# One decoder layer on one core: score products not pinned, the mixers' norm weight spread by products, first loads rearranged

## The chip, the core and the metric

The kernel runs on one core of a Trainium2 chip. The time is that of one execution on the device in microseconds; three runs of the kernel before gave 1481.52 to 1482.3, median 1482.07. The core has five engines, each with an instruction stream of its own that it works off in order: PE (products and transposes), ACT (activations and copies), DVE and POOL (element-wise work) and SP, which here issues loads. They wait for each other through semaphores. SP, ACT and POOL each feed a DMA queue; all three are served by the same sixteen DMA engines.

## What is computed

A hybrid decoder layer on 512 tokens of width 1024: RMSNorm, one input projection whose columns are split between four retention heads and a sliding-window attention with eight query heads, an output projection, then a mixture of 32 experts (four for each token), an embedding gate and a last RMSNorm. Cut to the part that matters here:

```python
hn = rmsnorm(h, g_mix_norm[i])
u = hn @ w_in[i] + b_in[i]
rq, rk, rv, rg, aq, ak, av = split_cols(u, IN_SIZES)
ret = retention(rq, rk, rv, positions)     # rope on q and k, chunks of 128 tokens
ret = jax.nn.silu(rg) * rmsnorm(ret, ret_norm_g[i])
att = sliding_window_attention(aq, ak, av, att_sinks[i], rel_bias_table)
h = h + jnp.concatenate([ret, att], axis=-1) @ w_out[i]
h = h + moe(rmsnorm(h, g_moe_norm[i]), ...)
```

## The kernel before

The mixers take the first 240 us or so; the mixture of experts behind them takes nearly all the rest and is not touched. All of the mixers works on four tiles of 128 tokens.

*Start.* The four tiles of x (`xt`) and the norm's weight `g_mix`, which a DMA spreads from one row over 128 partitions, come in by SP's queue, and so do the weights. A weight piece (`raw`, 128x2048, 1 MB) is loaded by `prefetch()` into one of three buffers as soon as one is free; the list `pieces` gives their order: two pieces of head 0, one of the attention's keys and values (`w_kv`), two of its queries, two for each further head. In the order of SP's queue stand x's tile 0, g_mix, piece 0, x's tile 1, piece 1, x's tiles 2 and 3, `w_kv`. For each tile ACT sums the squares (L287), DVE makes the factor 1/rms from it in a chain of small operations (L257 to L273, with a square root on ACT) and the normalised tile xn (L362); PE transposes it in two halves (L301), and ACT and DVE take each half out of PSUM, ACT as a rounded part `act_h` (L292) and DVE as the remainder `act_l` (L293).

*Weights* are split in the same manner: ACT writes the rounded part `wh` (L151), DVE the remainder `wl` (L152), for head 0 in quarters of 128x512, else as a whole. A product is made of three: wh by act_h, wh by act_l and wl by act_h.

*Rotary tables* (`rotary_tables`, L436 to L464): DVE works out the angles from the positions in 18 operations, and ACT takes the sine and cosine.

*A retention head* (`retention(h)`, L523): two weight pieces; then for two groups of two tiles each: 24 products a tile (L316) into one of two PSUM buffers (`mm`), DVE adds the bias into `u` (L538, which frees the buffer), POOL makes the sine part of the rotation `rb` (L546), DVE the cosine part and their sums `ra` (L549, L554), PE transposes ra (L558), ACT evicts it (L560); scores and state on PE (L575, L583), score times values (L578), queries times the state before (L580: the cross product); squares on ACT (L593), a chain of fourteen small operations on DVE to `y` (L257 to L598, with the gate: Silu on ACT, L566, times the norm's weight `rng_b` on POOL, L567), two transposes of y (L601) and their eviction.

*The attention* (`attention_in`, L408; `attention(nb)`, L466) works by blocks of 128 queries. For each half of the heads four score products of depth 64 (L482) are made, two of them on the lower and two on the upper half of the partitions (kv = 0, 1), into one PSUM tile for each half; `tc.issue_after` pins each behind the one before, so that the halves alternate. DVE, ACT (Exp) and PE do the softmax and the product with the values.

The program calls head 0, the attention's inputs, block 0, head 1, blocks 1 and 2, head 2, block 3, head 3. The framework's scheduler sets the order of each engine's instructions from the program by costs and due times of its own; `tc.issue_after(x)` adds that what is issued inside stands behind x.

Of the kernel before, what the change touches and what calls it, by code (L numbers as in the profile page):

```python
# [11 lines left out]
F32 = mybir.dt.float32  # L12
# [83 lines left out]
def hymba_kernel(ctx, tc, x, p, positions, rel_bias_table, g_mix_norm, w_in, b_in, ret_norm_g,  # L96
# [58 lines left out]
    def w_half(w, k0, c0):  # L155
        def load(t):
            nc.sync.dma_start(out=t.rearrange("p (k c) -> p k c", k=4),
                              in_=w[k0 * P:(k0 + 4) * P, c0:c0 + 512].rearrange("(k p) c -> p k c", p=P))
        return load
# [2 lines left out]
        nc.sync.dma_start(out=t.rearrange("p (k c) -> p k c", k=8),  # L162
                          in_=w_in[:, 2560:2816].rearrange("(k p) c -> p k c", p=P))

    def w_ret(h, k0):
        def load(t):
            tv = t.rearrange("p (k s c) -> p k s c", k=4, s=4)
            src = w_in[k0 * P:(k0 + 4) * P, :].rearrange("(k p) c -> p k c", p=P)
            for s in range(4):
                c0 = s * 512 + h * P  # L170
                nc.sync.dma_start(out=tv[:, :, s, :], in_=src[:, :, c0:c0 + P])
        return load

    def expert_of(w, t):
# [22 lines left out]
        nc.sync.dma_start(out=t.rearrange("p (k c) -> p k c", k=2),  # L197
                          in_=w_ple_proj.rearrange("(k p) c -> p k c", p=P))

    pieces = [w_ret(0, 0), w_ret(0, 4), w_kv, w_half(w_in, 0, 2048), w_half(w_in, 4, 2048)]  # L200
    for h in range(1, HR):
        pieces += [w_ret(h, 0), w_ret(h, 4)]
    n_first = len(pieces)
# [14 lines left out]
    def prefetch(after=None):  # L218
        if free and state["next"] < min(len(pieces), state["limit"]):
            t, pl_ = raw_tile()  # L220
            if after is not None:
                nc.scalar.activation(t[:, 0:1], after[:, 0:1], AF.Copy)
            pieces[state["next"]](t)
            queue.append((t, pl_))
            state["next"] += 1

    def next_piece(parts=None, dst=None, more=True):
        t, pl_ = queue.pop(0)
        r = split(t, parts, dst)
        free.append(pl_)  # L230
        if more:
            prefetch()
        return r
# [9 lines left out]
    def bcast(pl_, src, n, name, eng=None, bufs=1):  # L243
        t = pl_.tile([P, n], F32, name=name, bufs=bufs)
        (eng or nc.gpsimd).dma_start(out=t, in_=src.rearrange("(o n) -> o n", o=1).broadcast_to([P, n]))
        return t
# [48 lines left out]
    def split_t(tp, src, hi, lo, n=KD):  # L295

        for g in range(0, n, 4):
            m = min(4, n - g)
            t = tp.tile([P, 4, P], F32, name="tp")
            for j in range(m):  # L300
                R.tr = nc.tensor.transpose(out=t[:, j, :], in_=src[:, (g + j) * P:(g + j + 1) * P], identity=ident)  # L301
            ins = split_ps(t[:, 0:m, :], hi[:, g:g + m, :], lo[:, g:g + m, :])
        return ins
# [39 lines left out]
    n1 = pool(nx, "n1", 2)  # L343
    xts = [n1.tile([P, D], F32, name="xt", bufs=NT) for _ in range(NT)]
    nc.sync.dma_start(out=xts[0], in_=x_v[:, 0, :])
    g_mix = bcast(n1, g_mix_norm[0], D, "g_mix", nc.sync)
    prefetch()
    nc.sync.dma_start(out=xts[1], in_=x_v[:, 1, :])
    prefetch()
    for i in range(2, NT):  # L350
        nc.sync.dma_start(out=xts[i], in_=x_v[:, i, :])
    warm = small.tile([P, 1], F32, name="warm", bufs=1)
    nc.vector.memset(warm, 1.0)
    nc.scalar.activation(warm, warm, AF.Sqrt)
    nc.scalar.dma_start(out=cst[:, P:C_REV], in_=consts[:, P:C_REV])
    nc.gpsimd.dma_start(out=pos_i, in_=positions[0].rearrange("(i p) -> p i", p=P))
    sink_b = bcast(const, att_sinks[0], 8, "sink_b")

    for i in range(NT):
        r = rstd(sumsq(xts[i], n1.tile([P, D], F32, name="xn")), D, 1, table=True)  # L360
        xn = n1.tile([P, D], F32, name="xn")
        nc.vector.scalar_tensor_tensor(xn, in0=xts[i], scalar=r, in1=g_mix, op0=ALU.mult, op1=ALU.mult)  # L362
        split_t(tp, xn, xh[:, :, i * P:(i + 1) * P], xl[:, :, i * P:(i + 1) * P])
    prefetch()
    nx.close()

# [8 lines left out]
    av = at.tile([P, NT, P], F32, name="av")  # L375
    aqT = at.tile([P, 4, S], F32, name="aqT")
    rng_b = rp.tile([P, 512], F32, name="rng_b", bufs=1)
    nc.gpsimd.dma_start(out=rng_b, in_=ret_norm_g.rearrange("o h d -> o (h d)").broadcast_to([P, 512]))

    def side_tables():  # L380

# [84 lines left out]
    def attention(nb):  # L466
        nk = 1 if nb == 0 else 2
        k0 = max(nb - 1, 0) * P
        o_sb = at2.tile([P, 512], F32, name="o_sb", bufs=1)
        o_ps = flat(oap.tile([P, 4, P], F32, name="o_ps")).rearrange("p (h d) -> p h d", d=64)  # L470
        sm = small.tile([P, 8], F32, name="sm")
        mx = small.tile([P, 8], F32, name="mx")
        nmx = small.tile([P, 8], F32, name="nmx")
        kvs = [slice(kv * 64, kv * 64 + 64) for kv in range(2)]
        for gp in range(2):

            s_ps = [sps.tile([P, 512], F32, name="s_ps").rearrange("p (a b) -> p a b", a=2) for _ in range(2)]
            m = None
            for g in range(2):
                for kv, rows in enumerate(kvs):  # L480
                    with tc.issue_after(m.ins) if m is not None else nullcontext():
                        m = nc.tensor.matmul(s_ps[kv][:, g, 0:nk * P], lhsT=aqT[rows, gp * 2 + g, nb * P:(nb + 1) * P],  # L482
                                             rhs=akT[rows, k0:k0 + nk * P], start=True, stop=True)
            for kv, rows in enumerate(kvs):
                h0 = kv * 4 + gp * 2
                h2_ = slice(h0, h0 + 2)
                s_sb = at2.tile([P, S], F32, name="s_sb").rearrange("p (a b) -> p a b", a=2)
                nc.vector.scalar_tensor_tensor(
                    s_sb[:, :, 0:nk * P], in0=s_ps[kv][:, :, 0:nk * P], scalar=0.125,
                    in1=band[:, h2_, 256 - nk * P:256], op0=ALU.mult, op1=ALU.add)  # L490
                nc.vector.tensor_reduce(out=mx[:, h2_], in_=s_sb[:, :, 0:nk * P], op=ALU.max, axis=AX.X)
                nc.vector.tensor_tensor(out=mx[:, h2_], in0=mx[:, h2_], in1=sink_b[:, h2_], op=ALU.max)
                nc.vector.tensor_scalar(nmx[:, h2_], mx[:, h2_], -1.0, None, op0=ALU.mult)
                for g in range(2):
                    c = h0 + g
                    nc.scalar.activation(s_sb[:, g, 0:nk * P], s_sb[:, g, 0:nk * P], AF.Exp, bias=nmx[:, c:c + 1],
                                         accum_out=sm[:, c:c + 1])
                t = tp.tile([P, 4, P], F32, name="tp")
                for g in range(2):
                    for kb in range(nk):  # L500
                        nc.tensor.transpose(out=t[:, g * nk + kb, :], in_=s_sb[:, g, kb * P:(kb + 1) * P], identity=ident)
                pT = at2.tile([P, 512], F32, name="pT").rearrange("p (a b) -> p a b", a=4)
                nc.any.tensor_copy(out=pT[:, 0:2 * nk], in_=t[:, 0:2 * nk])
                for g in range(2):
                    for kb in range(nk):
                        nc.tensor.matmul(o_ps[:, h0 + g, :], lhsT=pT[:, g * nk + kb, :],
                                         rhs=av[:, k0 // P + kb, rows], start=(kb == 0), stop=(kb == nk - 1))
        es = small.tile([P, 8], F32, name="es")
        nc.vector.tensor_tensor(out=es, in0=sink_b, in1=mx, op=ALU.subtract)
        nc.scalar.activation(es, es, AF.Exp)  # L510
        nc.vector.tensor_tensor(out=es, in0=es, in1=sm, op=ALU.add)
        nc.vector.reciprocal(out=es, in_=es)
        nc.vector.tensor_tensor(out=o_sb.rearrange("p (h d) -> p h d", d=64), in0=o_ps,
                                in1=es.rearrange("p (h o) -> p h o", o=1).broadcast_to([P, 8, 64]), op=ALU.mult)
        split_t(tp, o_sb, mix[nb][0][:, 4:8, :], mix[nb][1][:, 4:8, :], n=4)
# [6 lines left out]

    def retention(h):  # L523
        bias = rp.tile([P, 4, P], F32, name="bias")
        nc.gpsimd.dma_start(out=bias, in_=b_v[:, :, h * P:(h + 1) * P].broadcast_to([P, 4, P]))
        fine = [(lambda t, k=k: kslice(t, k), lambda t, k=k: kslice(t, k)) for k in range(4)] if h == 0 else None
        ws = [next_piece(fine), next_piece(fine)]
        r_prev = None
        for grp in range(2):
            i0 = grp * 2  # L530
# [12 lines left out]
            rbv = rb.rearrange("p i (a t d) -> p i a t d", a=2, t=2)  # L543
            i2 = slice(i0, i0 + 2)
            for t_o, t_i in ((0, 1), (1, 0)):
                nc.gpsimd.tensor_tensor(  # L546
                    out=rbv[:, :, :, t_o, :], in0=uv[:, :, :, t_i, :],
                    in1=sin[:, i2].rearrange("p i (o d) -> p i o d", o=1).broadcast_to([P, 2, 2, 64]), op=ALU.mult)
            nc.vector.tensor_tensor(  # L549
                out=ra.rearrange("p i (a d) -> p i a d", a=4), in0=u[:, :, 0:256].rearrange("p i (a d) -> p i a d", a=4),  # L550
                in1=cos[:, i2].rearrange("p i (o d) -> p i o d", o=1).broadcast_to([P, 2, 4, 64]), op=ALU.mult)
# [50 lines left out]
            for ii in range(2):  # L602
                split_ps(t[:, ii, :], mix[i0 + ii][0][:, h, :], mix[i0 + ii][1][:, h, :])

    rotary_tables()
    retention(0)
    side_tables()
    attention_in()
# [685 lines left out]
```

## Time and profile before

| | |
|---|---|
| median of three runs | 1482.07 us |
| the profiled execution's own time | 1484.27 us |
| its span | 1482.5 us |
| PE busy | 1352.3 us, 91% of the span |
| DVE busy | 830.4 us, 56% |
| ACT busy | 683.7 us, 46% |
| POOL busy | 211.1 us, 14% |
| mean granted clock of TensorE | 0.958 of full |
| PE busy, tenths, in the first eight of 40 slices | 5 9 9 9 9 8 7 9 |
| the same in the other 32 | 6 once, 8 three times, else 9 |

A slice is 37 us. The profiled execution took 2.2 us longer than the median of the runs; 1.8 us of its time lie around the span. Times in the rows below count from the start of the span.

### The profile page before, as it was taken

The page shows a single profiled execution, that of the slowest core. Times are in us where ns is not written, and L with a number is a line of the kernel's source. Part 1 is how long each engine was busy: PE and PEld are TensorE (multiplying, and loading weights), DVE is VectorE, ACT ScalarE, POOL GpSimd, SP SyncE. Part 2 cuts the span into 40 slices and gives each one's busy share as a digit, 9 for nine tenths or more (in the row PEclk, how much of TensorE's full clock was granted, in tenths as well). Part 3 has the DMA queues.
Part 4 walks back from the last instruction along what each step waited for, and adds up shares of the span by engine and source line. Part 5 has one row for each costly group of instructions (what it writes and reads, how often), then busy time and mean ns, then how long its engine had stood idle before and what let it go on. Part 6 is the DMA issues. An engine that isn't in the chain of part 4 may idle for free. (4 is left out here: it accounts for less than half of the span.)

```text
span 1482.5 us, 16876 instructions
## 1 busy us (share of the span) xinstructions
PE 1352.3 (91%) x6090; PEld 906.2 (61%) x6091; DVE 830.4 (56%) x1013; ACT 683.7 (46%) x754; POOL 211.1 (14%) x227
## 2 busy tenths in 40 slices
PE   5999987969899999999999999999999999999896
PEld 4776766757466564746555666474765675674275
DVE  6637663678456372645455656373664584573157
ACT  5334442356346262535445546263563563553154
POOL 2214130366201000000000000000000000100011
PEclk9999997979999999999999999999999999999998
DMA  9431036688799999999999999999999999999541
GB/s 272 119 108 29 1 116 245 206 281 338 292 401 390 410 399 410 399 395 402 399 386 404 391 380 391 395 398 375 401 380 369 365 385 367 362 347 365 199 147 57
DMA packets 110427, 462.47 MB, mean 312 GB/s; under 512 B 10830, under 2 KB 29180, under 8 KB 77568
## 3 DMA queue, kind: packets, MB, share of 16 engines
q1 hardware_dynamic: 99584, 436.24, 75.4%
q0 software_dynamic: 10320, 24.52, 6.6%
q8 instruction: 49, 0.80, 0.2%
q10 hardware_dynamic: 432, 0.57, 0.1%
q14 instruction: 42, 0.34, 0.1%
HBM read 447.26 MB, written 18.73 MB: 314 GB/s over the span
## 5 line engine op out<-in xcount | busy, mean ns | idle before, releaser
L152 DVE TENSOR_TENSOR wl<-raw,wh 128x2048 fp32r<-128x2048 f32 (+2 forms) x246 | 531.2, 2197 | 138.8 <-ACT wh L151 134.2
L151 ACT ACTIVATE wh<-raw 128x2048 fp32r<-128x2048 f32 (+2 forms) x246 | 444.3, 1839 | 108.4 <-PE up L854 55.8
L874 PE MATMUL up<-raw,xTh 128*64 128x512 f32 x896 | 198.6, 599 | 0.7 <-ACT xTh L823 0.7
L906 DVE TENSOR_SCALAR a<-up 128x512 f32<-128x512 f32 x50 | 34.5, 691 | 285.9 <-ACT sg L905 285.3
L854 PE MATMUL up<-wh,xTh 128*128 128x512 f32 x576 | 162.9, 404 | 14.5 <-ACT wh L151 13.0
L905 ACT ACTIVATE sg<-up 128x512 f32<-128x512 f32 x50 | 29.8, 597 | 302.8 <-issue 130.0
L854 PE MATMUL up<-wl,xTh 128*128 128x512 f32 x576 | 160.8, 400 | 2.3 <-DVE wl L152 2.3
L854 PE MATMUL up<-wh,xTl 128*128 128x512 f32 x576 | 160.9, 401 | 1.4 <-DVE xTl L293 1.4
L874 PEld LDWEIGHTS up<-raw,xTh 128*64 128x64 f32 x896 | 63.5, 138 | 126.8 <-issue 118.4
L854 PEld LDWEIGHTS up<-wh,xTh 128*128 128x128 f32 x576 | 108.1, 191 | 45.7 <-ACT wh L151 18.3
L854 PEld LDWEIGHTS up<-wl,xTh 128*128 128x128 f32 x576 | 108.6, 190 | 33.2 <-DVE wl L152 7.5
L854 PEld LDWEIGHTS up<-wh,xTl 128*128 128x128 f32 x576 | 109.7, 191 | 28.8 <-DVE xTl L293 2.1
L938 PE MATMUL dn<-wh,aTh 128*128 128x512 f32 x288 | 99.5, 429 | 23.1 <-ACT wh L151 23.1
L938 PE MATMUL dn<-wl,aTh 128*128 128x512 f32 x288 | 103.6, 444 | 12.4 <-DVE wl L152 12.4
L874 PE MATMUL dn<-raw,aT 128*64 128x512 f32 x448 | 104.8, 607 | 3.1 <-PEq L1055 3.1
L952 POOL DMA_INDIRECT acc<-y,slot_i x30 | 45.5, 1515 | 432.4 <-ACT y L947 418.9
L807 POOL DMA_INDIRECT xe<-xg,slot_i x30 | 34.0, 1132 | 503.4 <-PE dn L867 240.6
L938 PE MATMUL dn<-wh,aTl 128*128 128x512 f32 x288 | 97.5, 422 | 0.0
L938 PEld LDWEIGHTS dn<-wh,aTh 128*128 128x128 f32 x288 | 58.2, 207 | 42.1 <-ACT wh L151 26.6
L938 PEld LDWEIGHTS dn<-wl,aTh 128*128 128x128 f32 x288 | 58.1, 212 | 30.3 <-DVE wl L152 17.2
L947 ACT ACTIVATE y<-dn,slots 128x1024 f32<-128x1024 f32 (+1 forms) x30 | 27.5, 916 | 98.6 <-PE dn L938 52.3
L924 DVE SCALAR_TENSOR_TENSOR aTl<-tp,aTh 128x512 fp32r<-128x512 f32 x36 | 23.9, 688 | 81.1 <-ACT aTh L923 81.1
(340 smaller groups left out, 1598.4 us busy)
## 6 DMA issues: line engine op xcount, KB each, us to landing
raw<-in_w_up_dram SPq DMA_DIRECT2D x256, 1024.0 KB, 14.7
raw<-in_w_down_dram SPq DMA_DIRECT2D x128, 1024.0 KB, 12.9
raw<-in_w_in_dram SPq DMA_DIRECT2D x32, 256.0 KB, 3.9
raw<-in_w_out_dram SPq DMA_DIRECT2D x4, 1024.0 KB
raw<-in_w_ple_gate_dram SPq DMA_DIRECT2D x4, 1024.0 KB, 11.6
raw<-in_w_in_dram SPq DMA_DIRECT2D x3, 1024.0 KB, 5.2
xt<-in_x_dram SPq DMA_DIRECT2D x4, 512.0 KB, 8.5
h<-in_x_dram POOLq DMA_DIRECT2D x4, 512.0 KB, 5.7
```

The lines of the kernel that those rows point to most:

```text
L151: R.split_act = nc.scalar.activation(to(wh), src(raw), AF.Copy)
L152: R.split_dve = nc.vector.tensor_tensor(out=to(wl), in0=src(raw), in1=to(wh).bitcast(F32), op=ALU.subtract)
L807: return nc.gpsimd.indirect_dma_start(out=dst[0:n, 0:D // h], out_offset=None, in_=xg.rearrange("s (h d) -> (s h) d", h=h), in_offset=bass ...
L854: nc.tensor.matmul(h[n // 2][:, n % 2 * 512:n % 2 * 512 + 512], lhsT=a[:, k, :], rhs=w[:, n * 512:(n + 1) * 512], start=(k == 0 and a is x ...
L874: R.pair = nc.tensor.matmul(o[v * 64:v * 64 + 64, c:c + 512], lhsT=xT[:, k, :], rhs=w[:, v * n + c:v * n + c + 512], start=False, stop=las ...
L905: nc.scalar.activation(sg, hv[:, :, 0], AF.Silu, scale=ALPHA)
L906: nc.vector.tensor_scalar(a[:, cs], hv[:, :, 1], LIMIT + 1.0, 1.0 - LIMIT, op0=ALU.min, op1=ALU.max)
L924: nc.vector.scalar_tensor_tensor(flat(l[:, g4, :]), in0=flat(t), scalar=1.0 / ALPHA, in1=flat(h[:, g4, :]).bitcast(F32), op0=ALU.mult, op1 ...
L938: m = nc.tensor.matmul(o[:, n * 512:(n + 1) * 512], lhsT=a[:, k, :], rhs=w[:, kk * 1024 + n * 512:kk * 1024 + (n + 1) * 512], start=False, ...
L947: nc.scalar.activation(y[:, 0:o.shape[1]], o, AF.Copy, scale=gate)
L952: nc.gpsimd.indirect_dma_start(out=acc.rearrange("s (h d) -> (s h) d", h=h), out_offset=bass.IndirectOffsetOnAxis(ap=idx[0:n, :], axis=0), ...
```

## The change

1. *Norm weight.* The row g_mix_norm is loaded once to one partition (`g_row`); two products with a row of ones (L360 of the changed kernel) spread it into PSUM, and ACT copies it to `g_mix` (L361).
2. *Two queues.* Head 0's second weight piece is loaded by POOL's queue in four DMAs; x's tiles 1 to 3 stand directly behind the first piece on SP's queue.
3. *Loads behind the first rotation.* The loads of `rng_b` and of head 1's bias, on POOL's queue, are issued after head 0's first rotation (`R.rot`).
4. *Pins at the start.* The rotary tables stand behind xn of tile 0 (`R.xn`), the splits of head 0's weights behind the evictions of tile 0 (`R.x_hi`, `R.x_lo`).
5. *Scores.* The pins between the score products are gone.

```diff
-    def w_ret(h, k0):
+    def w_ret(h, k0, eng=None):
...
-                nc.sync.dma_start(out=tv[:, :, s, :], in_=src[:, :, c0:c0 + P])
+                (eng or nc.sync).dma_start(out=tv[:, :, s, :], in_=src[:, :, c0:c0 + P])
...
-    pieces = [w_ret(0, 0), w_ret(0, 4), w_kv, w_half(w_in, 0, 2048), w_half(w_in, 4, 2048)]
+    pieces = [w_ret(0, 0), w_ret(0, 4, nc.gpsimd), w_kv, w_half(w_in, 0, 2048), w_half(w_in, 4, 2048)]
...
-    g_mix = bcast(n1, g_mix_norm[0], D, "g_mix", nc.sync)
+    g_row = n1.tile([1, D], F32, name="g_row", bufs=1)
+    nc.sync.dma_start(out=g_row, in_=g_mix_norm[0].rearrange("(o n) -> o n", o=1))
     prefetch()
-    nc.sync.dma_start(out=xts[1], in_=x_v[:, 1, :])
-    prefetch()
-    for i in range(2, NT):
+    for i in range(1, NT):
         nc.sync.dma_start(out=xts[i], in_=x_v[:, i, :])
...
+    one = n1.tile([1, P], F32, name="one", bufs=1)
+    nc.vector.memset(one, 1.0)
+    g_mix = n1.tile([P, D], F32, name="g_mix", bufs=1)
+    for c in range(2):
+        ps = mm.tile([P, 512], F32, name="mm")
+        nc.tensor.matmul(ps, lhsT=one, rhs=g_row[:, c * 512:(c + 1) * 512], start=True, stop=True)
+        nc.scalar.activation(g_mix[:, c * 512:(c + 1) * 512], ps, AF.Copy)
     nc.gpsimd.dma_start(out=pos_i, in_=positions[0].rearrange("(i p) -> p i", p=P))
+    prefetch()
...
+        if i == 0:
+            R.xn, R.x_lo, R.x_hi = m, m2, R.hh
...
-    nc.gpsimd.dma_start(out=rng_b, in_=ret_norm_g.rearrange("o h d -> o (h d)").broadcast_to([P, 512]))
...
-            m = None
             for g in range(2):
                 for kv, rows in enumerate(kvs):
-                    with tc.issue_after(m.ins) if m is not None else nullcontext():
-                        m = nc.tensor.matmul(s_ps[kv][:, g, 0:nk * P], lhsT=aqT[rows, gp * 2 + g, nb * P:(nb + 1) * P],
-                                             rhs=akT[rows, k0:k0 + nk * P], start=True, stop=True)
+                    nc.tensor.matmul(s_ps[kv][:, g, 0:nk * P], lhsT=aqT[rows, gp * 2 + g, nb * P:(nb + 1) * P],
+                                     rhs=akT[rows, k0:k0 + nk * P], start=True, stop=True)
...
-        nc.gpsimd.dma_start(out=bias, in_=b_v[:, :, h * P:(h + 1) * P].broadcast_to([P, 4, P]))
+        with tc.issue_after(R.rot.ins) if h == 1 else nullcontext():
+            nc.gpsimd.dma_start(out=bias, in_=b_v[:, :, h * P:(h + 1) * P].broadcast_to([P, 4, P]))
...
-        ws = [next_piece(fine), next_piece(fine)]
+        with tc.issue_after(R.x_lo.ins), tc.issue_after(R.x_hi.ins):
+            ws = [next_piece(fine), next_piece(fine)]
...
+            if h == 0 and grp == 0:
+                with tc.issue_after(R.rot.ins):
+                    nc.gpsimd.dma_start(out=rng_b, in_=ret_norm_g.rearrange("o h d -> o (h d)").broadcast_to([P, 512]))
...
-    rotary_tables()
+    with tc.issue_after(R.xn.ins):
+        rotary_tables()
```

With these the scheduler orders the mixers anew on all engines. In three places the order is shown as the program has it.

ACT at the start, before (xt is a tile of x, tp a transposed half, raw a weight piece):

```order
L287 ACTIVATE xn,ss<-xt 128x1024
L259 ACTIVATE rs_y_146<-rs_v_145 128x1
L655 ACTIVATE sel<-cst 128x2
L151 ACTIVATE wh<-raw 128x512
L292 ACTIVATE act_h<-tp 128x4x128
L151 ACTIVATE wh<-raw 128x512
L292 ACTIVATE act_h<-tp 128x4x128
L287 ACTIVATE xn,ss<-xt 128x1024
```

and now:

```order
L287 ACTIVATE xn,ss<-xt 128x1024
L259 ACTIVATE rs_y_155<-rs_v_154 128x1
L667 ACTIVATE sel<-cst 128x2
L361 ACTIVATE g_mix<-mm 128x512 x2
L287 ACTIVATE xn,ss<-xt 128x1024
L259 ACTIVATE rs_y_183<-rs_v_182 128x1
L292 ACTIVATE act_h<-tp 128x4x128 x2
L287 ACTIVATE xn,ss<-xt 128x1024
L151 ACTIVATE wh<-raw 128x512 x2
```

The sum of tile 1 and its square root have moved ahead of the evictions of tile 0, and the sum of tile 2 ahead of the first weight split; before, the first weight split stood directly behind tile 0's square root.

DVE around head 0's first u, before:

```order
L152 TENSOR_TENSOR wl<-raw,wh 128x512
L266 SCALAR_TENSOR_TENSOR rs_t_203<-rs_y_202,rs_v_201 128x1
L152 TENSOR_TENSOR wl<-raw,wh 128x512
L272 TENSOR_SCALAR rs_t_203<-rs_t_203 128x1
L273 TENSOR_TENSOR rs_y_202<-rs_y_202,rs_t_203 128x1
L362 SCALAR_TENSOR_TENSOR xn<-xt,rs_y_202,g_mix 128x1024
L538 TENSOR_TENSOR u<-mm,bias 128x512
L152 TENSOR_TENSOR wl<-raw,wh 128x2048
```

and now (qkT, y, sin and cos are the rotary tables' tiles here):

```order
L465 SCALAR_TENSOR_TENSOR sin<-y,qkT 128x256
L464 TENSOR_SCALAR y<-y 128x256
L466 SCALAR_TENSOR_TENSOR sin<-y,sin 128x256
L465 SCALAR_TENSOR_TENSOR cos<-y,qkT 128x256
L467 SCALAR_TENSOR_TENSOR sin<-y,sin 128x256
L466 SCALAR_TENSOR_TENSOR cos<-y,cos 128x256
L470 TENSOR_SCALAR sin<-sin 128x256
L467 SCALAR_TENSOR_TENSOR cos<-y,cos 128x256
L546 TENSOR_TENSOR u<-mm,bias 128x512
L469 TENSOR_SCALAR cos<-cos 128x256
L546 TENSOR_TENSOR u<-mm,bias 128x512
```

The first two u stood among the weight remainders, behind the normalised tile 2, with the rotary tables long done; now all four tiles, all remainders and sixteen of the eighteen rotary operations stand ahead of them.

PE at head 3, from the cross product (or_ps<-r_prev,qkT) to the second transposes of ra, before:

```order
L580 MATMUL or_ps<-r_prev,qkT 128x128
L316 MATMUL mm<-wh,act_h 128x512
L316 MATMUL mm<-wh,act_l 128x512 x4
L316 MATMUL mm<-wl,act_h 128x512 x4
L601 MATMUL tp<-cst,y 128x128 x2
L558 MATMUL tp<-cst,ra 128x128 x4
```

and now:

```order
L591 MATMUL or_ps<-r_prev,qkT 128x128
L316 MATMUL mm<-wl,act_h 128x512 x3
L316 MATMUL mm<-wh,act_h 128x512 x4
L316 MATMUL mm<-wh,act_l 128x512 x4
L316 MATMUL mm<-wl,act_h 128x512 x4
L316 MATMUL mm<-wh,act_h 128x512 x4
L316 MATMUL mm<-wh,act_l 128x512
L612 MATMUL tp<-cst,y 128x128 x2
L316 MATMUL mm<-wh,act_l 128x512 x3
L316 MATMUL mm<-wl,act_h 128x512 x4
L569 MATMUL tp<-cst,ra 128x128 x4
```

Nine products stood between the cross product and y's transposes and none behind these; now twenty stand between and seven behind. At head 2 it was 20 products between and none behind, and is 27 and none.

## Rows read from the trace of the kernel before

**Rows 1.** Busy time by stretch: us, engines busy (count), PEclk, DMA share, GB/s.

```profile
0.00:10.00 10.00, 0.00 (x0) 0.01 (x1) 1.28 (x11) 2.94 (x7) 5.71 (x18) 1.00 0.81 227
10.00:20.00 10.00, 4.73 (x13) 3.18 (x14) 7.96 (x26) 4.57 (x10) 0.00 (x0) 1.00 1.11 321
...
180.00:190.00 10.00, 10.00 (x45) 7.00 (x44) 4.71 (x21) 1.80 (x8) 0.00 (x0) 0.83 0.00 0
```

**Rows 2.** ACT timeline, the start: start us, us, line, tiles, [idle before <-releaser].

```profile
4.53 1.06 ACT L287 ACTIVATE xn<-xt 128x1024 f32<-128x1024 f32 x1 [1.83 <-DMA xt<-in_x_dram]
...
14.82 0.63 ACT L151 ACTIVATE wh<-raw 128x512 fp32r<-128x512 f32 x1 [5.40 <-DMA raw<-in_w_in_dram]
```

**Rows 3.** DVE timeline, the start.

```profile
8.80 0.24 DVE L439 CAST pos_f<-pos_i 128x4 f32<-128x4 int32 x1 [7.91 <-DMA pos_i<-in_positions_dram]
...
13.66 0.42 DVE L458 SCALAR_TENSOR_TENSOR cos<-y,cos 128x256 f32<-128x256 f32 x1
...
27.28 1.28 DVE L362 SCALAR_TENSOR_TENSOR xn<-xt,rs_y,g_mix 128x1024 f32<-128x1024 f32 x1
28.48 0.68 DVE L538 TENSOR_TENSOR u<-mm,bias 128x512 f32<-128x512 f32 x1
29.08 2.28 DVE L152 TENSOR_TENSOR wl<-raw,wh 128x2048 fp32r<-128x2048 f32 x1
31.28 1.28 DVE L293 TENSOR_TENSOR act_l<-tp,act_h 128x512 fp32r<-128x512 f32 x2
```

**Rows 4.** PE timeline, head 0 and the key/value products.

```profile
33.46 1.09 PE L316 MATMUL mm<-wh,act_h 128*128 128x512 f32 x4
34.39 1.10 PE L316 MATMUL mm<-wh,act_l 128*128 128x512 f32 x4
...
40.37 0.63 PE L558 MATMUL tp<-cst,ra 128*128 128x128 f32 x4 [0.46 <-DVE act_l L293]
...
44.18 0.39 PE L580 MATMUL or_ps<-r_prev,qkT 128*128 128x128 f32 x2
...
55.83 0.63 PE L558 MATMUL tp<-cst,ra 128*128 128x128 f32 x4 [1.46 <-DVE ra L554]
...
59.76 0.39 PE L580 MATMUL or_ps<-r_prev,qkT 128*128 128x128 f32 x2
...
64.51 0.41 PE L601 MATMUL tp<-cst,y 128*128 128x128 f32 x2 [0.40 <-DVE y L598]
```

**Rows 5.** PE timeline, score products of blocks 1, 2 and 3.

```profile
141.94 0.70 PE L482 MATMUL s_ps<-akT,aqT 64*128 64x256 f32 x2
...
145.64 0.70 PE L482 MATMUL s_ps<-akT,aqT 64*128 64x256 f32 x4
...
188.82 1.13 PE L482 MATMUL s_ps<-akT,aqT 64*128 64x256 f32 x6
```

**Rows 6.** PE timeline, the waits of heads 2 and 3.

```profile
179.40 0.41 PE L601 MATMUL tp<-cst,y 128*128 128x128 f32 x2 [2.61 <-DVE y L598]
...
180.00 1.75 PE L316 MATMUL mm<-wh,act_h 128*128 128x512 f32 x4
...
206.60 0.60 PE L558 MATMUL tp<-cst,ra 128*128 128x128 f32 x4
...
210.31 0.39 PE L580 MATMUL or_ps<-r_prev,qkT 128*128 128x128 f32 x2
...
218.37 0.66 PE L601 MATMUL tp<-cst,y 128*128 128x128 f32 x2 [5.56 <-DVE y L598]
218.82 1.06 PE L558 MATMUL tp<-cst,ra 128*128 128x128 f32 x4
```

**Rows 7.** ACT timeline, the softmax of block 3.

```profile
196.40 1.28 ACT L566 ACT_TABLE_LOAD   x1
...
199.43 0.51 ACT L496 ACTIVATE s_sb<-s_sb,nmx 128x256 f32<-128x256 f32 x1
```

**Rows 8.** POOL timeline, the rotation of the last pair.

```profile
213.82 1.91 POOL L546 TENSOR_TENSOR rb<-u,sin 128x256 f32<-128x256 f32 x2 [0.16 <-DVE rs_w L278]
```

More of the change, by code (lines that the diff above doesn't have):

```diff
@@ L361, in hymba_kernel @@
         xn = n1.tile([P, D], F32, name="xn")
-        nc.vector.scalar_tensor_tensor(xn, in0=xts[i], scalar=r, in1=g_mix, op0=ALU.mult, op1=ALU.mult)
-        split_t(tp, xn, xh[:, :, i * P:(i + 1) * P], xl[:, :, i * P:(i + 1) * P])
+        m = nc.vector.scalar_tensor_tensor(xn, in0=xts[i], scalar=r, in1=g_mix, op0=ALU.mult, op1=ALU.mult)
+        m2 = split_t(tp, xn, xh[:, :, i * P:(i + 1) * P], xl[:, :, i * P:(i + 1) * P])
+        if i == 0:
+            R.xn, R.x_lo, R.x_hi = m, m2, R.hh
     prefetch()
@@ L545, in retention @@
             for t_o, t_i in ((0, 1), (1, 0)):
-                nc.gpsimd.tensor_tensor(
+                R.rot = nc.gpsimd.tensor_tensor(
                     out=rbv[:, :, :, t_o, :], in0=uv[:, :, :, t_i, :],
                     in1=sin[:, i2].rearrange("p i (o d) -> p i o d", o=1).broadcast_to([P, 2, 2, 64]), op=ALU.mult)
+            if h == 0 and grp == 0:
+                with tc.issue_after(R.rot.ins):
+                    nc.gpsimd.dma_start(out=rng_b, in_=ret_norm_g.rearrange("o h d -> o (h d)").broadcast_to([P, 512]))
             nc.vector.tensor_tensor(
```

## The prediction

> **What bounds the kernel now.** I read the stages first: the table at the front shows PE busy for 91% of the span, and nearly all the rest idle before 240 us, in the mixers; behind them PE is nine or more tenths busy in almost every slice. The edits stand in the mixers, and no load of the mixture of experts waits for anything that they touch but the mixers' end, so what they gain or lose there is carried to the end. Hence I price three places: the start, the score products, and the waits for a retention chain.
>
> At the start the loads rule: 2.27 MB arrive in 10 us, then 321 GB/s [rows 1]. ACT has tile 0's sum by 5.6, but DVE stands before the cast of the positions until 8.80 with tile 0's norm queued behind it; the first weight piece comes at 14.82 [rows 2, 3]. So what DVE does before 14.8 costs nothing, and the rotary tables are mostly done then (8.80 to 14.1). From there on DVE has work without a break: rows follow each other at 1.20 us (normalised tile), 0.60 (a 128x512 remainder or u) and 2.2 (a whole piece) [rows 3]. PE does a product in 0.235 us (four from 33.46 to 34.39) [rows 4]. The reader is to keep this in mind: **the rotary tables were free because they stood in a wait**.
>
> I count places by products (24 a tile, 96 a head). The first transposes of ra start at 40.37 with 66 products done, those of the second pair at 55.83 with 114 [rows 4].
>
> **The change, part by part.**
>
> *Loads.* The spread row leaves the SP queue (512 KB), and two loads (512 KB) go behind the first rotation; the second weight piece (1 MB) goes to POOL's queue, beside x's tiles. POOL issues four more DMAs, before it has anything to compute; none of its later work is needed before the rotation. Ahead of tile 1 stand x's tile 0, the first piece and the constants, 1.94 MB; with tile 1 2.46 MB, which by rows 1 is there at 10.6. If POOL's piece takes half, 2.98 MB are in by 12.2; if all of it goes first, 3.51 MB at 13.9. I take 11.4, between the first two, since before this POOL's queue first landed anything at 8.8 [rows 3]; 10.6 and 13.9 go to the range. The Trainium skill (DMA: Bandwidth & Descriptors, Queues, rings and completion order) says that a DMA engine goes round the queues that have work, a packet each. By that rule the halves hold, 12.2, and the sum below would be 0.8 us worse; no run here shows it yet.
>
> *ACT's order.* Tile 1's sum now stands ahead of tile 0's evictions, so these wait for tile 1's load: sum 11.4 to 12.5 [rows 2], evictions near 14, then tile 2's sum and the first weight split at some 16: a product about when it was before. What is late next is DVE.
>
> *DVE up to u.* Between tile 1's sum and the first u stand now: sixteen remainders of 128x512 (9.6), the key/value piece (2.2), three normalised tiles (3.6), three chains for their factors (2.4, an estimate at 0.2 us a small operation) and the sixteen operations of the rotary tables (4.0, at 0.25, from 8.80 to the last row near 14.1 less tile 0's work) [rows 3]. That is 21.8, and 1.8 of waits, for an eviction and for tile 3's transposes, which stand behind tile 1's last product: u at 12.5 + 21.8 + 1.8 = 36.1, before 28.48. PE's third tile needs the PSUM buffer that this u frees; it starts at 36.7, before 33.46. The gap of some five us will lower TensorE's clock as the one at 179.40 did; the seven products that stand next have until 40.2 and are not late at half speed.
>
> u of the second tile ends at 37.6, then small operations 0.6, ra 1.2, its two sums 0.8: transposes of ra at 40.2, but with 55 products done instead of 66. From there: 3.8 to the cross product (40.37 to 44.18), then y's chain, 4.75 (59.76 to 64.51) and one u more: y's transposes at 49.4 with 83 done. The 33 products to the next transposes of ra end at 57.6; the split of the next weights stands before ra on DVE and I give it 0.8: 58.4 with 116 done. Before, 116 was reached at 55.83 + 0.47 = 56.3 [rows 4]. **Start: +2.1.** With tile 1 at 10.6 or 13.9 it is +1.3 or +4.6.
>
> *Score products.* One product of 256 columns takes 0.70, two of different key halves together 0.70, three 1.13 [rows 5]: neighbours of different halves overlap, one more of the same half adds 0.43. Before, a group of four stood as one and three (1.83), once as 1, 2, 1 (2.10). Now two of one half stand together (1.13), or two and two (1.13 + 0.43 if the middle ones still overlap), and in block 2 six stand alone. Blocks 1 and 3: 1.13 + 1.56 + 1.13 = 3.82 each, before 3.66; block 2: 1.13 + 6 x 0.70 = 5.33, before 3.93. **+1.7**, on PE's path, since PE is full there; block 0 (narrow) stays within 0.2. Bounds 0 (the order of halves does not matter) and +2.6 (no overlap in the fours).
>
> *Waits for y in heads 2 and 3.* Taking the pins off lets the order change there. Head 2: PE waits 2.61 before y's transposes [rows 6] with 20 products between cross product and y; now 27. Seven fill 1.6 of the 2.61: **-1.6** (0 to -2.6). After that wait the granted clock is 0.83 over ten us [rows 1], four products take 1.75; after the wait of 1.46 the transposes took 0.63, no longer than elsewhere [rows 4, 6]. With about 1.0 left I expect no fall: 0.17 x 10 = **-1.7** (bounds 0 and -1.7).
>
> Head 3: ra's transposes at 206.60 with 511 products done, now 493: 18 x 0.235 = 4.2 earlier, 202.4. The cover for this is ACT: the softmax chain ahead had a table load, Silu and a table load in its middle, 196.40 to 199.43 [rows 7], which moved behind it. Without that cover PE idles the 4.2 away. Cross product 3.7 later at 206.1, 20 products and y (chain 4.75, now without u and ra in between) 211.2, seven products 213.2; u 0.6, the rotation on POOL 1.91 [rows 8], sums 0.8: second transposes of ra at 216.5 to 216.9, before 218.82 [rows 6]. **-2.1** (0 to -5.6, the whole wait before y).
>
> The two table loads fewer are ACT's and beside PE: nothing more.
>
> **Sum:** 2.1 + 1.7 - 1.6 - 1.7 - 2.1 = -1.6. Made on the profiled execution (1484.27) it gives 1482.7; on the median of the runs, which is 2.2 lower, **1480.5**. The order of all engines behind the mixers stays the same but for neighbours.
>
> **The rivals.**
>
> *Slower: the late gains stay out.* y's chain in head 2 now has u, ra and the rotation in its middle, as head 3's had before (210.31 to 218.37, 8.1 us, against 4.75 alone); if it grows as the filling does, and the softmax before head 3 is bound by DVE and not by the table loads, the last three terms are 0. Then +3.8: 1485.9, and 1488.4 with tile 1 at 13.9. It decides from 2 us of the 5.4. For it: the start's loss is fixed by the order. 0.25.
>
> *Faster: PE's waits before y close altogether.* -5.6 in the tail and -4.3 in head 2 with +3.8: 1476.0. It decides where 20 and 27 products cover the chain. Against it: ra of the last pair still needs the last product, then 3.3 us. 0.27.
>
> *The unpinned order costs nothing*, as PE overlaps halves in any order: 1478.8 with the rest as above. 0.08.
>
> *Forecast: given back*, 1478.0 to 1484.0 by itself: 0.40.
>
> **How the numbers follow.** A measurement of this kernel tells 0.2%, 3.0 us, from no change: faster is below 1479.1, slower above 1485.0. Faster: the faster case, half of the third and a little of the forecast's lower end, 0.33. Slower: most of the slower case, 0.22. The rest, 0.45. The range leaves one in ten at each end: 1475.5 to 1486.5.
>
> **What would show it.** Right: tile 1's sum before 13 us; the first u between 34.5 and 38; an idle PE ahead of the third tile; 116 products at 57 to 61; the scores' pairs at 1.1; less than 1.5 idle before y in head 2 and a clock of 1.00 behind; the last ra transposes early by two. Wrong: u before 32 (DVE has other waits to fill), or PE idle before y as long as before. The forecast fails as a whole if the start costs over 5 us, or if the mixers' end moves and the end of the program does not.

## The result and the profile after

The changed kernel took 1493.85 us (median of six runs, 1490.33 to 1494.6) against 1482.02 for the kernel before beside it: a ratio of 1.0078, interval 1.0065 to 1.009. It is slower by 11.8 us, and outside the range of 1475.5 to 1486.5.

Two views of the changed kernel, one behind the other, show the place. The first is busy time by stretch, with the columns of [rows 1].

```profile
10.00:20.00 10.00, 1.97 (x8) 1.57 (x8) 2.21 (x8) 3.10 (x6) 0.00 (x0) 1.00 1.06 344
...
40.00:50.00 10.00, 4.74 (x16) 3.31 (x16) 7.27 (x22) 4.30 (x6) 5.00 (x8) 0.66 0.12 28
...
190.00:200.00 10.00, 9.85 (x50) 7.24 (x49) 7.07 (x28) 4.56 (x14) 0.00 (x0) 1.00 0.00 0
```

DVE, busy for 7.96 us of the second ten before [rows 1], is busy for 2.21; PE stands for half of 40 to 50, where the granted clock is 0.66, between the two levels of 1.2 and 2.4 GHz. At 190 to 200, the stretch that answers to 0.83 before, it is 1.00.

The second view is the timeline of the start, all engines.

```profile
16.68 1.06 ACT L287 ACTIVATE xn<-xt 128x1024 f32<-128x1024 f32 x1 [7.59 <-DMA xt<-in_x_dram]
...
17.93 0.16 DVE L447 CAST pos_f<-pos_i 128x4 f32<-128x4 int32 x1
...
18.16 1.07 ACT L292 ACTIVATE act_h<-tp 128x512 fp32r<-128x512 f32 x2
...
21.83 0.78 PE L316 MATMUL mm<-wh,act_h 128*128 128x512 f32 x1
...
39.20 0.57 DVE L450 TENSOR_SCALAR qkT<-cst,pos_f 128x64 f32<-128x64 f32 x3
...
43.04 0.68 DVE L546 TENSOR_TENSOR u<-mm,bias 128x512 f32<-128x512 f32 x1
...
43.86 2.04 PE L316 MATMUL mm<-wh,act_h 128*128 128x512 f32 x4 [6.09 <-DVE u L546]
...
46.63 0.72 DVE L560 TENSOR_TENSOR ra<-u,cos 128x512 f32<-128x512 f32 x1 [0.98 <-ACT cos L472]
...
48.59 0.63 PE L569 MATMUL tp<-cst,ra 128*128 128x128 f32 x4 [1.40 <-DVE ra L565]
```

ACT stands 7.59 us before tile 1's load with tile 0's evictions (18.16) queued behind; DVE has nothing to do in that time, and the rotary tables, for which it was the right place, follow from 35 to 43, ahead of the first u. Before, they were nearly all done at 14.1 and u began at 28.48 [rows 3].

The PE timeline of the later places, to set beside [rows 4, 6]:

```profile
67.40 0.63 PE L569 MATMUL tp<-cst,ra 128*128 128x128 f32 x4 [1.77 <-DVE ra L565]
...
76.08 0.41 PE L612 MATMUL tp<-cst,y 128*128 128x128 f32 x2 [0.39 <-DVE y L609]
...
189.12 0.41 PE L612 MATMUL tp<-cst,y 128*128 128x128 f32 x2 [1.79 <-DVE y L609]
...
200.37 0.41 PE L612 MATMUL tp<-cst,y 128*128 128x128 f32 x2
...
211.11 1.10 PE L512 MATMUL o_ps<-av,pT 128*128 128x64 f32 x8 [0.94 <-DVE pT L509]
...
228.26 1.12 PE L569 MATMUL tp<-cst,ra 128*128 128x128 f32 x4 [3.81 <-DVE ra L565]
...
242.32 0.79 PE L308 MATMUL mm<-wh,raw 128*128 128x512 f32 x1 [2.80 <-ACT wh L151]
```

Read as a ledger: +11.1 at the second transposes of ra (67.40 with 116 products, before 56.3), +11.6 at y of head 0 (76.08 against 64.51), +9.4 at the last transposes of ra (228.26 against 218.82, 528 products in both), +9.5 at the first product of the output (242.32, before 232.82), which I call **the mixers' end**. The span is 10.3 longer. At y of head 0 two more products stand ahead than before (142 against 140), which is 0.5 of the 11.6 at 0.235 us a product. So the start lost 11.1, and what lies between it and the last transposes of ra gave back 1.7.

### The profile page after: what moved, and what is told of

Read it like the earlier page. It is cut to its first block, busy times and chain, and to the rows that moved or that the text cites. A ratio compares the mean times of both kernels' runs of the same rounds, so it can differ in the third digit from the quotient of the medians.

```text
span 1492.8 us, 16881 instructions
## 1 busy us (share of the span) xinstructions
PE 1356.1 (91%) x6094; PEld 908.1 (61%) x6095; DVE 831.8 (56%) x1016; ACT 681.2 (46%) x752; POOL 212.7 (14%) x231
## 5 line engine op out<-in xcount | busy, mean ns | idle before, releaser
L918 DVE TENSOR_SCALAR a<-up 128x512 f32<-128x512 f32 x50 | 34.5, 691 | 285.7 <-ACT sg L917 285.1
## 6 DMA issues: line engine op xcount, KB each, us to landing
raw<-in_w_ple_gate_dram SPq DMA_DIRECT2D x4, 1024.0 KB, 11.8
```

Source lines behind the costliest of these rows:

```text
L918: nc.vector.tensor_scalar(a[:, cs], hv[:, :, 1], LIMIT + 1.0, 1.0 - LIMIT, op0=ALU.min, op1=ALU.max)
```

## The experiments

Runs of one and the same kernel spread by several us (the kernel before from 1478 to 1486 over all its runs), so I also read the place of the mixers' end in the trace; what lies behind it up to the end of the span was 1246 to 1252 us in every run, without an order by kernel. Each place comes from a single trace, and how far it moves from one execution to the next was not measured, so differences of about one us decide nothing. All of it:

| run | ratio to before, interval | tile 1's sum | first u | mixers' end, less 232.8 |
|---|---|---|---|---|
| the change | 1.0078, 1.0065 to 1.009 | 16.68 | 43.04 | +9.5 |
| e1 load back | 1.0019, 1.0006 to 1.0032 | 17.94 | 30.97 | +2.9 |
| e2 spread alone | 1.0048, 1.0032 to 1.0063 | 13.53 | 41.30 | +8.7 |
| e3 spread alone, elsewhere | 0.9998, 0.9988 to 1.0009 | 15.64 | 25.95 | -0.3 |
| e4 loads as before | 1.0042, 1.0028 to 1.0055 | 13.45 | 38.50 | +6.5 |
| e5 one queue | 1.0046, 1.0029 to 1.0063 | 12.35 | 38.78 | +5.0 |
| e6 evictions first | 1.0057, 1.0041 to 1.0074 | 17.00 | 40.43 | +8.1 |
| e7 scores alone | 0.9986, 0.9976 to 0.9995 | 17.16 | 28.29 | -2.5 |
| e8 elsewhere, no pins | 0.9986, 0.9976 to 0.9995 | 17.78 | 30.30 | -1.2 |
| e9 unused 4.5 KB alone | 1.0037, 1.0024 to 1.0051 | 14.57 | 39.45 | +6.5 |
| e10 elsewhere, pins kept | 1.0051, 1.0031 to 1.0072 | 16.67 | 37.51 | +4.4 |
| e11 elsewhere, no pins, one queue | 0.9994, 0.9982 to 1.0007 | 15.18 | 28.09 | -0.4 |
| e12 spread elsewhere, scores | 1.0005, 0.9989 to 1.0021 | 16.14 | 25.53 | -2.5 |
| e13 elsewhere, tables' pin only | 1.004, 1.0024 to 1.0056 | 17.62 | 33.17 | +5.3 |
| e14 elsewhere, splits' pin only | 1.0004, 0.9992 to 1.0015 | 16.41 | 33.12 | +0.7 |
| e15 no pins, memory kept | 1.0072, 1.0047 to 1.0098 | 17.66 | 41.73 | +9.3 |

**The spread of the norm weight: load, products, or memory.** The sizes in the code led to a suspicion. The inputs' pool holds 16 KB a partition of x, two work tiles (8) and the weight (4): 28 KB. The row takes 4 KB of every partition though only one is used, the ones 0.5. The pools that are opened when the inputs' pool is closed hold 30 KB (20 and 10) before the rotary tables. With 28 the tables lie behind the inputs; with 32.5 they lie on them, and have to wait for their readers. The sum comes from the code; no run varied the size around 30.

e1 puts the broadcast load back into the changed kernel:

```diff
-    g_row = n1.tile([1, D], F32, name="g_row", bufs=1)
...
+    g_mix = bcast(n1, g_mix_norm[0], D, "g_mix", nc.sync)
```

> The changed kernel with one part undone: the norm weight comes spread over the partitions by its 512 KB load again, no row, no products. Theory A (memory): the row and the ones took 4.5 KB a partition beside the inputs (28 KB before, now 32.5), the retention's pools start 30 KB behind the same base, so the rotary tables lie where tile 3's normalisation still reads and DVE does 16 of their 18 operations and all eight activation remainders ahead of the first u. Undone, all 18 stand in the early wait again: first u near 30, second transposes of ra near 58 with 119 products done, 1480 to 1484. Theory B (loads): tile 1 came at 16.7 because the second weight piece and tiles 2 and 3 share the way; 512 KB more make it later: first u 40 or later, 1492 or more.

The ratio is 1.0019, with u at 30.97, though tile 1 came later still (17.94). 6.6 of the 9.5 are back. Theory A holds in the main: the sine's half of the tables stands in the early wait (9.57 to 14.3), the cosine's mostly at 19 to 23. The time came out above what A gave (1485.6).

e2 makes the spread alone in the kernel before, e3 the same with the two small tiles in memory that the mixers' output uses later (the output's four tiles are declared behind the norm for it):

```diff
-    g_row = n1.tile([1, D], F32, name="g_row", bufs=1)
+    spare = raw3.tile([P, 2048], F32, name="raw", tag="c3", bufs=1)
+    g_row = spare[0:1, 0:D]
...
-    one = n1.tile([1, P], F32, name="one", bufs=1)
+    one = spare[0:1, D:D + P]
```

> The kernel before with one part alone: the norm weight spread by products from one row, both small tiles beside the inputs; loads, queues and pins as before. Theory A (memory): the tables stand behind all four tiles again, first u at 36 to 43, 1489 to 1494. Theory B (loads): 512 KB less stand ahead of the first piece and tile 1, tile 1 near 14.5, 1479 to 1483. Theory C (the products themselves, four passes of 0.94 us in single precision, hold up tile 0's norm): like A here.

> As the run before, but the row and the ones lie in one of the four 8 KB tiles that the mixers' output uses later, so that the inputs' pool keeps its size; the products are the same. Theory A (memory): the tables stand in the early wait, the order around u is that of the kernel before, first u 27 to 31, 1479 to 1484. Theory C (the products): no better than the run with both tiles beside the inputs, 1489 to 1494.

With its small tiles in the one place the spread costs 8.7 us at the mixers' end, in the other nothing. Theory B falls with e2 (tile 1 there by 13.5 at the latest, and u still at 41.30), C with e3. e9 is the run without any product, with an unused tile in the kernel before:

```diff
+    pad = n1.tile([1, 1152], F32, name="pad", bufs=1)
+    nc.vector.memset(pad[:, 0:1], 0.0)
```

> The kernel before with nothing but an unused tile of 4.5 KB a partition in the inputs' pool (one element of it is set, one small DVE operation). Theory A (memory): the order is that of the run with the spread by products alone, tables behind all four norms, first u near 41, 1488 to 1492. Theory C (the products and their evictions): no change, 1481 to 1484.

The mixers end 6.5 later by a tile that nobody reads; the 2.2 between this and e2 were not taken apart. Its DVE timeline shows the order that the memory leads to, without anything else in the way:

```profile
8.74 0.17 DVE L441 CAST pos_f<-pos_i 128x4 f32<-128x4 int32 x1 [7.81 <-DMA pos_i<-in_positions_dram]
...
31.37 1.28 DVE L364 SCALAR_TENSOR_TENSOR xn<-xt,rs_y,g_mix 128x1024 f32<-128x1024 f32 x1
32.57 0.25 DVE L444 TENSOR_SCALAR qkT<-cst,pos_f 128x64 f32<-128x64 f32 x1
...
39.02 0.42 DVE L461 SCALAR_TENSOR_TENSOR cos<-y,cos 128x256 f32<-128x256 f32 x1
39.45 0.69 DVE L540 TENSOR_TENSOR u<-mm,bias 128x512 f32<-128x512 f32 x1
```

The positions are there at 8.74 as before, but the first operation of the tables starts at 32.57, at the very end of the last tile's norm (31.37 + 1.28), the last reader of the inputs' pool on DVE.

**The second queue.** e4 undoes the whole of part 2 of the change, the queue and the order of the loads; e5 undoes only the queue. Part 3, the loads behind the first rotation, stays in both and was not run by itself.

```diff
-    pieces = [w_ret(0, 0), w_ret(0, 4, nc.gpsimd), w_kv, ...
+    pieces = [w_ret(0, 0), w_ret(0, 4), w_kv, ...
```

> The changed kernel with the loads undone: the second weight piece on SP's queue behind tile 1, tiles 2 and 3 behind it, as before; row, products and pins stay. Theory A (memory): the first u still stands behind the tables and all four norms; tile 1 lands at 13 to 15 as 512 KB less stand ahead, 1487 to 1493. Theory B (loads): the loss goes with tile 1's landing, 1481 to 1485.

> The changed kernel with the second weight piece on SP's queue, at its place behind the inputs' tiles; nothing else. It tells what held tile 1 until 16.7. If the piece on POOL's queue took the way from tile 1: tile 1 at 13.0 to 14.0, all that follows 3 earlier, 1489 to 1491. If it is tiles 2 and 3, issued right behind tile 1: tile 1 stays at 16 to 17 and the second piece comes later, 1493 to 1496.

e4 came out as A said: tile 1's sum at 13.45, u at 38.50. ACT and DVE of e5:

```profile
12.35 1.06 ACT L287 ACTIVATE xn<-xt 128x1024 f32<-128x1024 f32 x1 [2.83 <-DMA xt<-in_x_dram]
```
```profile
38.78 0.69 DVE L546 TENSOR_TENSOR u<-mm,bias 128x512 f32<-128x512 f32 x1
```

It came out by the first branch. Without the piece on POOL's queue tile 1 is there 4.3 us earlier, more than the 3 expected; u moves by 4.3 and the mixers' end by 4.5. So the queue did take the way from tile 1; but +5.0 are left, with tile 1 within 1 us of where the forecast had it.

**ACT's order.** e6 pins the sums of tiles 1 to 3 behind tile 0's evictions:

```diff
-        r = rstd(sumsq(xts[i], n1.tile([P, D], F32, name="xn")), D, 1, table=True)
+        with tc.issue_after(R.x_hi.ins) if i else nullcontext():
+            ss = sumsq(xts[i], n1.tile([P, D], F32, name="xn"))
+        r = rstd(ss, D, 1, table=True)
```

> The changed kernel with one pin more: the sums of tiles 1 to 3 stand on ACT behind tile 0's evictions, which so no longer wait for tile 1's load; the tables stay behind all four norms. If DVE's work from tile 1's sum to u is what counts: first product near 16 instead of 21.8, but u only 2 to 4 earlier (39 to 41), 1490 to 1492. If ACT's wait for tile 1 is what counts: u 5 to 6 earlier with the first product, 1486 to 1489.

The first product is at 18.72 (later than expected: the first weight split follows tile 1's sum), u is 2.6 earlier, the mixers' end only 1.4. What counts is DVE's row of work behind tile 1's sum, not ACT's wait.

**The scores.** e7 takes the pins off the score products of the kernel before.

> The kernel before with the score products not pinned, nothing else: the start stays (116 products at 56.3), the scores cost 1.0 to 1.7, heads 2 and 3 gain 3 to 4 as in the changed kernel (wait for y in head 2 1.8 instead of 2.6, in head 3 3.8 before ra instead of 5.6 before y). Mixers' end 1.5 to 2.5 earlier, 1479.5 to 1481. If the late gains of the changed kernel came from its late start instead, nothing here: 1482 to 1484.

The mixers end 2.5 earlier, at a ratio of 0.9986: the late gain belongs to the scores' order, not to the late start. Its PE timeline:

```profile
177.37 0.41 PE L599 MATMUL tp<-cst,y 128*128 128x128 f32 x2 [1.79 <-DVE y L596]
...
199.36 1.10 PE L504 MATMUL o_ps<-av,pT 128*128 128x64 f32 x8 [0.92 <-DVE pT L501]
...
216.53 0.82 PE L556 MATMUL tp<-cst,ra 128*128 128x128 f32 x4 [3.81 <-DVE ra L552]
```

The same waits as in the changed kernel, 1.79 and 3.81; a new one of 0.92, for DVE, stands in front of head 3.

**The pins on tile 0.** The change also holds the tables behind tile 0's norm and the first weight splits behind tile 0's split. e8, e10, e13 and e14 have the row elsewhere and neither pin, both, or one; e15 has no pins with the row beside the inputs; e11 is e8 with one queue. The pins:

```diff
-    with tc.issue_after(R.xn.ins):
-        rotary_tables()
+    rotary_tables()
...
-        with tc.issue_after(R.x_lo.ins), tc.issue_after(R.x_hi.ins):
-            ws = [next_piece(fine), next_piece(fine)]
+        ws = [next_piece(fine), next_piece(fine)]
```

> The changed kernel with the row and the ones in the later tile of the mixers' output, and the two pins on the first tile's norm and splits undone; queues, loads behind the rotation and unpinned scores stay. Theory A (memory): tables in the early wait, first u near 28 to 31, start within 2 of the kernel before, late gain of 2: 1478 to 1483. If the second queue is what costs, tile 1 still lands at 16 to 17 and holds DVE's order: 1486 to 1490.

> The changed kernel with the row and the ones in the later tile of the mixers' output; the two pins, queues and all else stay. If memory alone moved the tables: 1479 to 1483, as without the pins. If the pins and tile 1's late load cost by themselves: DVE's cast of the positions and the tables stand behind tile 1's sum at 16.7, first u at 37 to 40, 1485 to 1490.

> The changed kernel with the row and the ones elsewhere and the pin on the first weight splits undone; the pin of the tables behind tile 0's norm stays. With both pins the mixers end at 237.2, without both at 231.6. If the splits' pin exposed tile 1's late load: mixers' end 231 to 233, 1480 to 1483. If it was the tables' pin: 236 to 238, 1486 to 1489.

> The counterpart: the row elsewhere, the tables' pin undone, the splits' pin kept. If the tables' pin was the cost: mixers' end 231 to 233, 1480 to 1483. If the splits' pin was: 236 to 238, 1486 to 1489.

> The changed kernel with both pins undone, the row and the ones beside the inputs as in the change. If memory and pins add up: mixers' end near 236.8 (242.3 less 5.5), 1486 to 1489. If the memory alone holds the tables behind all four norms, the pins cost nothing here: 241 to 243, 1491 to 1494.

> As the run with the row elsewhere and no pins, but the second weight piece on SP's queue: tile 1 at 12 to 13. If tile 1's landing still matters without the pins: 1477 to 1479.5, faster than both kernels. If DVE then waits for the weight pieces alone: 1480 to 1482, no better than the run before it.

At the mixers' end, with the row elsewhere: no pins -1.2, the splits' pin +0.7, the tables' pin +5.3, both +4.4. It is the tables' pin: e10 and e13 came out by their second branch, e14 by its first, half a microsecond above the 233 given. The first u does not tell this by itself: it stands at 33.17 in e13 and at 33.12 in e14, but y of head 0 at 71.36 and at 67.13. With the pin PE's order behind u is another one too, and how its cost divides between the tables' place and that order is open. The two rows of y, e13 first:

```profile
71.36 0.41 PE L612 MATMUL tp<-cst,y 128*128 128x128 f32 x2 [1.55 <-DVE y L609]
```
```profile
67.13 0.41 PE L613 MATMUL tp<-cst,y 128*128 128x128 f32 x2 [0.39 <-DVE y L610]
```

With the row beside the inputs: +9.3 without pins, +9.5 with both. So they do not add up: the memory moves the tables further than the pin does, and hides it. The waits of DVE in e8 and in the changed kernel, up to 60 us (line, what it waited for: total, times, longest), show what was lost:

```profile
DVE pos_f L448 <- DMA pos_i<-in_positions_dram: 6.8, 1, 6.8
DVE wl L152 <- ACT wh L151: 3.3, 1, 3.3
```
```profile
DVE rs_v L257 <- ACT xn L287: 12.3, 2, 7.5
DVE act_l L293 <- ACT act_h L292: 3.0, 2, 2.4
```

In e8 DVE waits for the positions first, and can fill the time up to the weights with the tables. In the changed kernel it waits for ACT's sums of tiles 0 and 1 (12.3), and the tables stand behind both. The pin alone does not forbid them the second of these waits: in e10, with the memory free, tile 0's norm ends at 10.57, and yet the cast of the positions stands at 17.92, directly behind the first operation on tile 1's sum. That is the order which the scheduler chose. DVE in e10:

```profile
9.28 1.29 DVE L369 SCALAR_TENSOR_TENSOR xn<-xt,rs_y,g_mix 128x1024 f32<-128x1024 f32 x1 [2.32 <-ACT g_mix L361]
17.85 0.15 DVE L257 TENSOR_SCALAR rs_v<-ss 128x1 f32<-128x1 f32 x1 [7.28 <-ACT xn L287]
17.92 0.16 DVE L448 CAST pos_f<-pos_i 128x4 f32<-128x4 int32 x1
```

With the tables in their place the second queue shows no cost: e11 has one queue and does not end earlier than e8 (0.8 later). Tile 1's landing was dear because DVE's whole row stood behind it.

**Together.** e12 is the kernel before with the spread elsewhere and the scores not pinned.

> The kernel before with two parts of the change: the spread by products with its tiles elsewhere, and the score products not pinned. The two runs of one part each add up: start as before, heads 2 and 3 2.5 earlier, 1479.5 to 1481.5. If the late gain needs another start: 1482 to 1484.

The mixers end 2.5 earlier, as in e7, but the time shows no gain (1.0005). The traces allow no more than that the spread brings nothing. e8 and e11, which have the loads of the change besides, end 1.3 and 2.1 later than e12, so those loads show no gain either. Faster than both kernels by its interval is e7, the score products without pins and nothing else, and e8 by as much.

## Why the prediction was wrong

It failed in one large step and four smaller ones; together they make 11.0 of the 13.4 us between the forecast of 1480.5 and the measured 1493.85. The other 2.3 lie behind the mixers' end, where the runs differ by more than that (1246 to 1252), and stay open.

**Tile 1's landing**, taken at 11.4 with 13.9 as the worst, was 16.7: +5.3. I counted the bytes ahead of it and divided by the rate. The order of e5 has no second queue in the way, and there too it came at 12.35 where that count, without the piece, gives 10.6; with POOL's piece it came 2.8 after the end that let the whole piece go first. By the rule of the Trainium skill (DMA: Bandwidth & Descriptors, Queues, rings and completion order) the two queues share, and my estimate from it was 12.2. The trace has 16.7, so neither that estimate nor mine gives the landing here. A load's landing cannot be had from the bytes ahead of it alone: 4.4 MB had moved by then (190 GB/s to 4.95, 253 to 10, 301 to 14, 380 to 16.7), where all that could stand ahead by my count is 3.5.

**DVE up to u**, 21.8 of work and 1.8 of waits behind the end of tile 1's sum: it took 25.3 (17.74 to 43.04), +1.7; the waits were larger, 2.40 of them before tile 3's eviction.

**From u to ra's transposes**, 4.1 in the forecast, 5.55 measured: a wait was not in the sum. The cosine table ends on ACT, behind a table load, and ra stood 0.98 for it. With the tables moved behind the other work, ACT's part of them moved too.

**From there to 116 products** it took 18.8 against 18.2. These four make the 9.0 between the 58.4 of the forecast and 67.40.

**The scores and heads 2 and 3** gave 1.7 instead of 3.7. Block 2 came as forecast, two products of one half at 1.13 and six alone at 0.70. In blocks 1 and 3 the four in the middle took 1.34 together, where I had 1.56: 3.60 a block, before 3.66. That is +1.3 instead of +1.7. The clock did not fall behind head 2's wait, as forecast: the stretch from the transposes of ra there (179.65) to the next of y (192.09) took 12.44 us before and 11.02 in e7, with 57 PE instructions in both. But the wait there closed by 0.8, not 1.6 (1.79 left), and head 3 gave 0.7 where 2.1 was the forecast. (From the y at 192.09, now 200.37, to the last transposes of ra it is 26.73 before and 27.89 now, with eight more products to do, which are 1.9.) The 5.56 became 0.94 and 3.81, the second before ra itself, as the argument against the faster rival had said. The stretch in the kernel before and in e7, with the columns of [rows 1], and the y before:

```profile
179.65:192.09 12.44, 12.44 (x57) 8.88 (x55) 6.57 (x28) 4.03 (x11) 0.00 (x0) 0.86 0.00 0
```
```profile
177.61:188.63 11.02, 10.87 (x57) 7.94 (x55) 7.43 (x28) 5.21 (x16) 0.54 (x1) 1.00 0.00 0
```
```profile
192.09 0.40 PE L601 MATMUL tp<-cst,y 128*128 128x128 f32 x2
```

**The signs.** Right were the idle PE ahead of the third tile (6.09), the scores' pairs at 1.13, the clock of 1.00 behind head 2 and the last transposes of ra earlier than the start's loss, by 1.7 of the 2 expected; wrong were tile 1's sum, u (43.04, not 34.5 to 38), 116 products at 67.40 (57 to 61) and the 1.79 left before y.

**The rivals.** The slower one had the right sign and the wrong place: it let the late gains stay out, and they came. What the list of signs named as the end of the forecast, a start that costs over 5 us, is what happened. "The rotary tables were free because they stood in a wait" was right. I priced their move at their own 4.0 us on DVE, since I took the new order as given and asked only how long its instructions take. Why the tables stand there I did not ask, and so never saw that 4.5 KB and one pin cost the largest part: with the loads, the scores and the spread kept, and only the tiles' place and the pins undone, the mixers end 10.7 us earlier (e8).

## What to carry to other kernels

- A tile of one partition takes its bytes in all of them. Before adding a small tile to a pool that is closed early, add up which later tiles will lie on it; an unused 4.5 KB cost 0.37% here.
- Work that is free because it fills a wait must keep two things: its place in the order and memory that is free at that time. Its own length does not price its loss: the tables are 4.0 us of DVE, and their pin cost 6.5 at the mixers' end (e13 against e8), with a wait of 7.5 left empty in the changed kernel.
- Calibrate a forecast of a load's landing on a load of the same trace, and let the bound go beyond the sum of the bytes.

## What was not expected of the hardware

The second queue's megabyte held a tile of 512 KB back by 4.3 us (12.35 to 16.68), more than the 2.8 to 3.5 that its bytes would take at the 301 to 380 GB/s of the stretch before 16.7. What share each queue had is open: no run varied the size of the packets or the piece.

Four score products in two halves, two and two, took 1.34 us, hardly more than two of one half (1.13), as these rows of the changed kernel's PE timeline show (each product is two records):

```profile
142.35 1.13 PE L488 MATMUL s_ps<-akT,aqT 64*128 64x256 f32 x4
...
144.05 1.34 PE L488 MATMUL s_ps<-akT,aqT 64*128 64x256 f32 x8
```

And a product from one row is not short: the two of the spread, of 512 columns each, took 3.75 us on PE at the start (4.70 to 8.45 in the changed kernel). In e3 that cost nothing at the mixers' end.
